# Four projection chunks of a two-layer encoder in Strassen-Winograd form, with the gates kept transposed in DRAM

## The chip, the core and the metric

The kernel runs on one core of a Trainium2 chip. The metric is the device time of one launch, in microseconds (us). The engines are named as the profile names them: PE is TensorE (PEld its weight loads), DVE is VectorE, ACT is ScalarE, POOL is GpSimd, SP is SyncE, which issues every DMA of this kernel. SBUF is the on-chip working memory, PSUM the banks that PE writes to.

## What is computed

Two encoder layers on 1024 tokens of width 1024, all in float32. Each layer normalises, projects once, runs two kinds of attention side by side, gates them, projects back and adds:

```python
proj = rms_norm(x, pre_norm_g[l]) @ w_in[l]              # 1024 x 3328
aq, ak, av, ag, bq, bk, bv, bg = split(proj)             # 512 each, but bk and bv 128 each
oa = diff_attention(aq, ak, av, lam, rel_bias)           # 4 heads, two softmaxes per head
ya = rms_norm(oa, diff_subln_g[l]) * (1 - lam_init) * silu(ag)
yb = gqa_attention(rope(rms(bq)), rope(rms(bk)), bv) * silu(bg)   # 8 query heads on 2 key heads
x = x + rms_norm(concat(ya, yb) @ w_out[l], post_norm_g[l])
```

## The kernel before, in words

**Arithmetic.** Every matmul operand is split into two parts, `hi` (rounded by a copy on ACT) and `lo` (the rest, a subtraction on DVE or POOL). A product is three matmuls: hi by hi, hi by lo, lo by hi (`mm3`). A chunk of 512 projected columns over 1024 rows of depth and 1024 tokens is 8 x 8 x 3 = 192 matmuls of 128 x 512.

**The normalised tokens.** `hT` holds them transposed: for each half of the tokens (`th`) and each half of the depth (`kh`) a pair of hi and lo tiles, 8 tiles in all. With the depth halves as columns and the token halves as rows this is a 2 by 2 block matrix, which the change uses.

**Stages of a layer.** Key/value and query chunks of group B come first, then the chunks `aq` and `ak` (`col_chunk`: the weights are the stationary operand, so the result comes out transposed), then the gates `ag` and `bg` and the values `av` (`tok_chunk`: the tokens are stationary, one PSUM tile per 128 tokens). `gate_post` puts the SiLU of a gate into the row tile `ys[t]`, and for group A multiplies it with `gsub`, the attention norm's gain. Weights are loaded 1 MB at a time into `h` tiles and split into `w` tiles (`w_steps`), the lo half mostly on POOL.

**Attention** goes item by item in `tick`: one tick takes the next item's scores on PE, the reduction of the current one on DVE, its exponential on ACT, later its transposes and its product with the values. `after(d, fn)` puts `fn` off by `d` ticks. The ticks at the start have spare PE work in `fill`: the last two token tiles of `av`, 48 matmuls in five portions, with `av_post` one tick behind (`FD = 1`). The finished rows are multiplied into `ys[t]`, where the gate already lies.

**The end of attention.** `y_transposed(t)` transposes a finished row tile in two halves through the two `pT` banks and splits each. Those of tiles 0 and 1, and the split of the output weights, are laid among the last ticks (`ENDING`); tile t + 2 goes with step t of the first half of the output projection.

**What sets the order.** PE is kept in program order everywhere (`inorder`). In the attention ticks DVE, ACT and POOL are too. Elsewhere a scheduler orders the other engines, SP always, and gives out buffers from pools: 10 `h`, 8 `w`, 6 `e`, 8 `y` tiles, two `pS`, two `pO` and two `pT` places in PSUM. Each engine then runs its list strictly in order: an instruction that waits holds up all behind it.

Of the kernel before, what the change touches and what calls it, by code (L numbers as in the profile page):

```python
# [51 lines left out]
def hybrid_encoder(ctx, tc, x, rel_bias, pre_norm_g, w_in, diff_lambda, diff_subln_g,  # L52
# [208 lines left out]

    def lambdas_of(l, dl):
        lam_init = 0.8 - 0.6 * math.exp(-0.3 * l)
        gsub = cst.tile([P, P], F32, tag="gsub", name=f"gsub{l}")
# [9 lines left out]
        nc.sync.dma_start(gsub, bcast_row(diff_subln_g[l:l + 1, :], P))  # L274
        dve.tensor_scalar(gsub, gsub, 1.0 - lam_init, None, ALU.mult)
        return gsub, neglam

# [25 lines left out]
    def layer(l, hT, ends, given):  # L303
# [7 lines left out]
        bk_d = d_tile([P, 2, 2, S], f"bk_d{l}")  # L311
        bv_d = d_tile([P, 2, NT, P], f"bv_d{l}")

        ys = [None] * NT
        tables = [None]

        def gate_post(t, gi, src):
            if ys[t] is None:
                ys[t] = y_tile()
            dst = ys[t][:, gi * 512:gi * 512 + 512]  # L320
            act.activation(dst, src, AF.Silu)
            if gi == 0:
                d4 = dst.rearrange("p (h c) -> p h c", c=P)
                g4 = gsub.rearrange("p (o c) -> p o c", o=1).broadcast_to([P, 4, P])
                dve.tensor_tensor(d4, d4, g4, ALU.mult)

        def rope_norm(src, t, nh, tab, eps, scale, dst):
            sq = e_tile((P, nh, 64))
# [93 lines left out]
                for fn in side.get(j, ()):  # L422
                    fn()

        def col_chunk(w, scale, store):
            for cb in range(4):
                pt = ps_s()
                for th in range(2):
                    mm_col(pt[:, th * 512:th * 512 + 512], hT[th], w, cb)
                    follow()  # L430
                hi = e_tile(dt=F32R)
                lo = e_tile(dt=F32R)
                act.activation(hi, pt, AF.Copy, scale=scale)
                dve.scalar_tensor_tensor(lo, pt, scale, f(hi), ALU.mult, ALU.subtract)
                store(cb, (f(hi), f(lo)))

        def store_q(h, parts):
            dst = aq_d[h].rearrange("d g (t x k) -> d (g t) x k", t=2, x=4)
            for i in range(2):
                for c in range(2):  # L440
                    nc.sync.dma_start(dst[:, :, 2 * i + c, :],
                                      parts[i][c * 64:c * 64 + 64].rearrange("d (t k) -> d t k", k=P))

        def store_k(h, parts):
            for i in range(2):
                nc.sync.dma_start(ak_d[h, i], parts[i])

        lo4, hi4 = range(4), range(4, 8)
        if l == 0:
# [80 lines left out]
            w_aq, loads, convs = w_steps(wl, C_AQ, on_dve=(1, 3))  # L530
# [4 lines left out]
        else:  # L535
# [6 lines left out]
            w_aq, loads, convs = w_steps(wl, C_AQ, on_dve=(1, 3))  # L542
# [6 lines left out]
        inorder[:] = [nc.tensor]  # L549
        tok_chunk(load_w(wl, C_AG), lambda t, s: gate_post(t, 0, s))  # L550
        tok_chunk(load_w(wl, C_BG), lambda t, s: gate_post(t, 1, s))
        warm = s_tile()
        inorder[:] = [nc.scalar]
        act.activation(warm, neglam, AF.Exp)
        inorder[:] = [nc.tensor]
        w_av = load_w(wl, C_AV)
        tok_chunk(w_av, av_post, tiles=range(NT - 2))

        now = [0]
        trans, parts, later_q, fill = [], [], [], []

        def fill_av(t, cuts):
            box = []

            def part(ks):
                if not box:
                    box.append(ps_o())
                for k in ks:  # L570
                    mm_k(box[0], hT, t, w_av, k)
                if ks[-1] == NK - 1:
                    after(FD, lambda: av_post(t, box[0]))
            fill.extend(lambda ks=ks: part(ks) for ks in cuts)

        for t, cuts in zip((NT - 2, NT - 1), FILL):
            fill_av(t, cuts)

        def after(delay, fn, mid=False):
            later_q.append((now[0] + delay, mid, fn))  # L580
# [96 lines left out]
        def a_out(h, g, aT, r0):  # L677
            box = []

            def part(i):  # L680
                if i == 0:
                    box.append(ps_o())
                pO = box[0][:, 0:256]
                V = values[h]
                for k in (2 * i, 2 * i + 1):
                    pe.matmul(pO, V[:, 0, k, :], aT[0][:, k, :], start=(k == 0), stop=False)
                    pe.matmul(pO, V[:, 0, k, :], aT[1][:, k, :], start=False, stop=False)
                    pe.matmul(pO, V[:, 1, k, :], aT[0][:, k, :], start=False, stop=(k == NK - 1))
                if i == 3:
                    after(0, lambda: finish(box[0]))  # L690

            def finish(pO):
                oT = o_tile((P, 256))
                act.copy(oT, pO[:, 0:256])
                p4 = pO[:, 256:512].rearrange("p (q c) -> p q c", c=P)
                ms = s_tile(2, "oms", 3)
                yv = [ys[g * 2 + qi][:, h * P:(h + 1) * P] for qi in range(2)]
# [49 lines left out]
        def b_out(hp, g, BV, bT, sr):  # L747
# [15 lines left out]
            def finish(j, pO, oT):  # L763
# [17 lines left out]
                def store():  # L781
                    for qi in range(2):
                        for jj in range(2):
                            c0 = 512 + hp * P + jj * 64
                            yv = ys[g * 2 + qi][:, c0:c0 + 64]
                            dve.scalar_tensor_tensor(yv, p4[:, qi, jj * 64:jj * 64 + 64],
                                                     sr[:, jj * 2 + qi:jj * 2 + qi + 1], yv, ALU.mult, ALU.mult)

            return [[lambda j=j, i=i: part(j, i) for i in range(2)] for j in range(2)]

# [10 lines left out]
        def load_ak(h):  # L801
            K = h_tile([P, 2, S], F32R)
            for i in range(2):
# [3 lines left out]
            nc.sync.dma_start(T5, bass.AP(tensor=rows_h.tensor, offset=rows_h.offset + 127,  # L807
                                          ap=[[2047, P], [1, 1920]]))
            return K, T5

        values = {}

# [12 lines left out]
        def all_items():  # L825
            for h in range(4):
# [9 lines left out]
                for g in range(4):  # L836
# [4 lines left out]
                    else:  # L841
                        for fn in half_loads:
                            fn()
                    if g == 0 and 0 < h < 3:
                        state["ak"] = load_ak(h + 1)
                    aT = new_probs()
# [241 lines left out]
```

## Time and profile before

| What | Value |
|---|---|
| Device time, median of three runs | 1461.31 us (1460.11 to 1461.55) |
| Profiled execution, device time | 1459.86 us |
| Its span, first to last instruction | 1457.8 us |
| PE busy | 98% of the span, 8300 matmuls |
| PEld, DVE, ACT, POOL busy | 86%, 57%, 53%, 50% |
| Granted PE clock | 1.00 |
| DMA | 162.45 MB, 111 GB/s on average |

The span is the time from the first to the last instruction; the device time of the same execution is 2.1 us more, for what lies around it. A matmul's end is modelled, so a row of matmuls is better judged by how far apart its members start than by its busy time. A busy share is a mean over stages that have different limits. The stages of the first layer, from the trace: group B's projections until 95 us, `aq` and `ak` until about 186, the gates until about 273, six tiles of `av` until 305, attention until 641, the output projection until 757. The second layer repeats them from there.

### The profile page before, as it was taken

Reading aid. Unit: us, or ns where it says so; the run is one execution under the profiler, and the core shown is the slowest. Engines: PE = TensorE matmul, PEld = TensorE weight load, DVE = VectorE, ACT = ScalarE, POOL = GpSimd, SP = SyncE. Lnnn points to the kernel's source line nnn. Section 1 sums busy time; section 2 is a strip of 40 time slices with the busy share of each in tenths; the row PEclk is TensorE's granted clock in tenths of the full one; section 3 lists DMA queues with packets and bytes.
Section 4 is the critical chain, followed back from the end, with each engine's and each line's share of the span. In section 5 each row is a group of like instructions: output and inputs, shape, how many; then the busy total and the mean of one; then the engine's idle time right before and its main releaser. Section 6 shows DMA issues by size and latency. Waiting matters only on the chain.

```text
span 1457.8 us, 22409 instructions
## 1 busy us (share of the span) xinstructions
PE 1427.4 (98%) x8300; PEld 1248.3 (86%) x8300; DVE 838.0 (57%) x1596; ACT 773.4 (53%) x1508; POOL 736.1 (50%) x740
## 2 busy tenths in 40 slices
PE   6999999999999999999999999999999999999998
PEld 6887888888999999988788888888899999998887
DVE  7861110048888888852786511100688888888423
ACT  5332122148888888852442222111688888888321
POOL 3541122018888888852333422020488888888320
PEclk9999999999999999999999999999999999999999
DMA  6488722165324222041525772124634142311303
GB/s 220 122 203 217 245 87 53 38 187 149 107 66 133 69 78 76 2 145 58 171 93 124 180 203 111 62 51 141 172 89 118 56 109 64 95 59 38 108 29 130
DMA packets 110669, 162.45 MB, mean 111 GB/s; under 512 B 8408, under 2 KB 72408, under 8 KB 108256
## 3 DMA queue, kind: packets, MB, share of 16 engines
q1 hardware_dynamic: 110560, 161.02, 38.2%
q8 instruction: 65, 1.06, 0.3%
q14 instruction: 44, 0.36, 0.1%
HBM read 112.72 MB, written 52.46 MB: 113 GB/s over the span
## 4 chain that ended last, share of the span: by engine, by line
PE 91%; DVE 4%; ACT 2%; issue 1%; POOL 1%; DMA 0%; POOLq 0%; DVEq 0%; SPq 0%; ACTq 0%
PE pS L65 40%; PE pO L65 39%; PE pT L65 13%; DVE y L65 2%; DVE h L65 1%; ACT w L65 1%; ACT e L65 1%; POOL e L65 0%; DVE s L65 0%; DVE w L65 0%; DMA e<-in_pre_norm_g_dram 0%; ACT h L65 0%; POOL w L65 0%; ACT o L65 0%; POOL s L65 0%
## 5 line engine op out<-in xcount | busy, mean ns | idle before, releaser
L65 PE MATMUL pO<-w,h 128*128 128x256 f32 (+1 forms) x3592 | 652.0, 330 | 0.3
L65 PEld LDWEIGHTS pO<-w,h 128*128 128x128 f32 x3592 | 567.1, 189 | 81.3 <-POOL w L65 0.9
L65 PE MATMUL pS<-h,h 128*128 128x512 f32 x1024 | 294.7, 410 | 0.0
L65 POOL TENSOR_TENSOR w<-h,w 128x1024 fp32r<-128x1024 f32 x53 | 127.2, 2421 | 266.8 <-ACT w L65 266.8
L65 PE MATMUL pT<-identr,e 128*128 128x128 f32 x1536 | 200.9, 273 | 1.1 <-DVE w L65 0.9
L65 PEld LDWEIGHTS pS<-h,h 128*128 128x128 f32 x1024 | 174.9, 190 | 24.5 <-ACT e L65 0.4
L65 PE MATMUL pS<-w,h 128*128 128x512 f32 (+1 forms) x912 | 195.3, 370 | 0.0
L65 DVE TENSOR_TENSOR w<-pT,w 128x512 fp32r<-128x512 f32 x256 | 169.7, 684 | 33.5 <-ACT w L65 33.5
L65 POOL TENSOR_SCALAR e<-e,s 128x1024 f32<-128x1024 f32 x64 | 71.8, 1122 | 229.9 <-DVE s L65 229.9
L65 PEld LDWEIGHTS pS<-w,h 128*128 128x128 f32 x912 | 159.3, 190 | 27.9
L65 PEld LDWEIGHTS pT<-identr,e 128*128 128x128 f32 x1536 | 172.6, 140 | 5.6 <-DVE w L65 4.8
L65 PE MATMUL pS<-h,w 128*128 128x512 f32 x768 | 177.0, 391 | 0.0
L65 POOL TENSOR_TENSOR s<-s,mhalf 128x2 f32<-128x2 f32 (+2 forms) x96 | 83.2, 867 | 184.5 <-DVE s L65 181.1
L65 POOL TENSOR_TENSOR w<-e,w 128x512 fp32r<-128x512 f32 x128 | 168.7, 1318 | 10.4
L65 PEld LDWEIGHTS pS<-h,w 128*128 128x128 f32 x768 | 143.5, 188 | 30.4 <-PE pO L65 0.5
L65 ACT CAST w<-pT 128x512 fp32r<-128x512 f32 x256 | 143.6, 587 | 46.2 <-PE pT L65 43.3
L65 DVE TENSOR_REDUCE s<-pS 128x1 f32<-128x1024 f32 x128 | 156.3, 1221 | 15.8 <-PE pS L65 15.0
L65 ACT ACTIVATE e<-e,s 128x1024 f32<-128x1024 f32 x128 | 148.2, 1158 | 22.9 <-DVE s L65 22.1
L65 DVE CUSTOM_DVE_ANT_0 e<-pS,h 128x1024 f32<-128x1024 f32 x128 | 155.6, 1217 | 5.9 <-PE pS L65 5.3
L65 POOL TENSOR_TENSOR e<-e,e 128x1024 f32<-128x1024 f32 x64 | 153.1, 2392 | 5.3
L65 ACT ACTIVATE e<-pS,s 128x1024 f32<-128x1024 f32 x128 | 144.6, 1130 | 6.8 <-issue 5.8
L65 ACT ACTIVATE o<-pO 128x128 f32<-128x128 f32 (+2 forms) x97 | 36.9, 381 | 127.5 <-PE pO L65 116.9
(76 smaller groups left out, 1081.8 us busy)
## 6 DMA issues: line engine op xcount, KB each, us to landing
h<-in_w_in_dram SPq DMA_DIRECT2D x52, 512.0 KB, 4.9
h<-aq_d SPq DMA_DIRECT2D x64, 256.0 KB, 5.2
bq_d<-y SPq DMA_DIRECT2D x64, 128.0 KB, 2.8
aq_d<-e SPq DMA_DIRECT2D x32, 256.0 KB, 4.4
ak_d<-e SPq DMA_DIRECT2D x16, 512.0 KB, 4.4
h<-bq_d SPq DMA_DIRECT2D x32, 256.0 KB, 5.9
h<-ak_d SPq DMA_DIRECT2D x16, 512.0 KB, 7.6
av_d<-e SPq DMA_DIRECT2D x32, 256.0 KB, 2.5
```

Source lines behind the costliest of these rows:

```text
L65: ins = fn(*args, **kw)
```

## The change

`aq`, `ak` and both gates, four chunks per layer, are computed as 2 by 2 block products in Winograd's form of Strassen's scheme. A block product that would take 8 half products (512 tokens by 256 columns over half the depth) takes 7, each of 2 x 4 x 3 = 24 matmuls. So a chunk has 168 matmuls and not 192, all with the weights stationary and the tokens moving.

- **Sums of the tokens** (`sum_steps`): DVE builds four sums `s1` to `s4` of the blocks of `hT` and splits them, during the `av` chunk, which now comes first and whole.
- **Sums of the weights** (`wino_steps`): each chunk's weights come in four loads of 512 KB, DVE forms their sums, and ACT and DVE split seven blocks `wb` of 128 x 4 x 256. POOL has no part in it.
- **Partial results**: products share PSUM (`a` and `b` in `pS` places, `c` in two `pO`), and DVE adds what has been kept in `y` tiles (`added`).
- **Order**: `av`, `ak`, `ag`, `bg`, `aq`. The last two steps of `aq`, 48 matmuls again, become the `fill` at the start of attention. In it `added` is called at once, and the post one tick later.
- **Gates** come out transposed and go to DRAM (`gate_d`) in 16 stores per layer; `load_gates` brings 1 MB per two row tiles back. Attention only copies its rows into `ys[t]`, and `y_transposed` multiplies the transposed rows with the gates (and with `gsub`, now one value per partition).

In all 192 matmuls are gone, 248 DVE and 76 ACT instructions are added (4 of these are table loads), 32 POOL instructions are gone, and 88 DMAs are added.

```diff
-FILL = ((range(0, 3), range(3, 6), range(6, 8)), (range(0, 4), range(4, 8)))
+FILL = (((5, 0, range(0, 3)),), ((5, 0, range(3, 4)), (5, 1, range(0, 2))), ((5, 1, range(2, 4)),),
+        ((6, 0, range(0, 4)),), ((6, 1, range(0, 4)),))
+WLD, WPR = 4, 2
...
+        def wino_steps(c0, post):
...
+            def parted(i, src):
+                wb[i] = w_tile([P, 2, 4, 256])
+                act.copy(wb[i][:, 0], src)
+                dve.tensor_tensor(wb[i][:, 1], src, f(wb[i])[:, 0], ALU.subtract)
...
+            def mm(i, cb, ks):
+                grp, x, first, _ = plan[i]
+                dst, (xh, xl) = bank(grp, cb), blocks[x]
+                cs = slice(cb * P, cb * P + P)
+                for k in ks:
+                    wh, wlo = wb[i][:, 0, k, cs], wb[i][:, 1, k, cs]
+                    on = dict(skip_group_check=not first)
+                    pe.matmul(dst, wh, xh[:, k, :], start=(first and k == 0), stop=False, **on)
+                    pe.matmul(dst, wh, xl[:, k, :], start=False, stop=False, **on)
+                    pe.matmul(dst, wlo, xh[:, k, :], start=False, stop=(k == 3), **on)
+
+            def added(grp, to, base, cb):
+                dst = kept(to, cb)
+                dve.tensor_tensor(dst, bank(grp, cb), kept(base, cb), ALU.add)
+                return dst
...
+            plan = [("a", "a11", True, p1),
+                    ("a", "a12", False, lambda cb: done(cb, 0, bank("a", cb))),
+                    ("b", "s2", True, lambda cb: added("b", "u2", "s1", cb) and None),
+                    ("b", "s3", False, lambda cb: added("b", "u3", "s1", cb) and None),
+                    ("b", "a22", False, lambda cb: done(cb, 1, added("b", "s1", "s1", cb))),
+                    ("c", "s1", True, lambda cb: done(2 + cb, 1, added("c", "u3", "u3", cb))),
+                    ("c", "s4", False, lambda cb: done(2 + cb, 0, added("c", "u2", "u2", cb)))]
...
-        col_chunk(w_aq, -0.125, store_q)
-        col_chunk(load_w(wl, C_AK), 1.0, store_k)
...
-        tok_chunk(load_w(wl, C_AG), lambda t, s: gate_post(t, 0, s))
-        tok_chunk(load_w(wl, C_BG), lambda t, s: gate_post(t, 1, s))
...
+        chunks = [wino_steps(C_AK, post_parts(1.0, store_k)), wino_steps(C_AG, post_gate(0)),
+                  wino_steps(C_BG, post_gate(1)), wino_steps(C_AQ, post_parts(-0.125, store_q))]
...
+        tok_chunk(w_av, av_post, side=side)
...
+        def fill_part(units):
+            for n, cb, ks in units:
+                more = chunks[3][2](n, cb, ks)
+                if more:
+                    after(FD, more)
...
                 def gate():
                     for qi in range(2):
-                        dve.tensor_tensor(yv[qi], p4[:, qi, :], yv[qi], ALU.mult)
+                        dve.tensor_copy(yv[qi], p4[:, qi, :])
...
         def y_transposed(t):
+            if t % 2 == 0 and t + 2 < NT:
+                load_gates(t // 2 + 1)
+            gate = gates[t // 2][:, :, (t % 2) * P:(t % 2) * P + P]
...
-                split(yT[0][:, sl, :], yT[1][:, sl, :], pT)
+                if kh == 0:
+                    dve.scalar_tensor_tensor(gate[:, sl, :], pT, gsub, gate[:, sl, :], ALU.mult, ALU.mult)
+                else:
+                    dve.tensor_tensor(gate[:, sl, :], pT, gate[:, sl, :], ALU.mult)
+                split(yT[0][:, sl, :], yT[1][:, sl, :], gate[:, sl, :])
```

**DVE at the start of attention.** This is DVE's list of the first layer before, from the second group-B reduction on. A row with `<-pS` is a reduction of scores (`ISA` with the bias added, `TENSOR_REDUCE` without), `w<-pT` the lo part of transposed probabilities, `e<-pO` the post of an `av` tile from the fill.

```order
L65 TENSOR_REDUCE s_2405<-pS_2386 128x1
L65 TENSOR_TENSOR e_2427<-pO_2353,e_2427 128x512
L65 ISA e_2444,s_2445<-pS_2407,h_2325 128x1024
L65 ISA s_2445 128x1
L65 TENSOR_TENSOR w_2365<-pT_2432,w_2364 128x4x128
L65 ISA e_2470,s_2471<-pS_2447,h_2325 128x1024
L65 ISA s_2471 128x1
L65 TENSOR_TENSOR e_2479<-pO_2412,e_2479 128x512
```

The same place after the change; `y<-pO` is `added` on a fill product, `e<-y` its post.

```order
L67 SCALAR_TENSOR_TENSOR e_2505<-y_2363,e_2505 128x512
L67 RECIPROCAL s_2440<-s_2442 128x2
L67 SCALAR_TENSOR_TENSOR s_2513<-s_2442,neglam_666,s_2440 128x1
L67 TENSOR_REDUCE s_2518<-pS_2491 128x1
L67 TENSOR_TENSOR y_2333<-pO_2456,y_2333 128x512
L67 SCALAR_TENSOR_TENSOR e_2540<-y_2363,e_2540 128x512
L67 ISA e_2559,s_2560<-pS_2520,h_2428 128x1024
L67 ISA s_2560 128x1
L67 TENSOR_TENSOR y_2333<-pO_2481,y_2333 128x512
L67 TENSOR_TENSOR w_2468<-pT_2547,w_2467 128x4x128
L67 SCALAR_TENSOR_TENSOR e_2584<-y_2333,e_2584 128x512
L67 ISA e_2593,s_2594<-pS_2562,h_2428 128x1024
```

The last fill product (`pO_2481`) is now read ahead of the reduction of `pS_2562`, the scores that PE makes just before that fill; before, the fill's post stood behind the corresponding reduction (`pS_2447`).

**DVE at the end of attention.** Before, from row tile 0's transposed halves (`h<-pT`) on; `w<-h` is the split of the output weights, `o<-o,pO` and `y<-pO` finish the last heads.

```order
L65 TENSOR_TENSOR h_6645<-pT_6646,h_6645 128x512
L65 TENSOR_TENSOR h_6645<-pT_6653,h_6645 128x512
L65 TENSOR_TENSOR o_6408<-o_6408,pO_6593 64x256
L65 RECIPROCAL s_6040<-s_6040 128x4
L65 SCALAR_TENSOR_TENSOR y_1805<-pO_6593,s_6040,y_1805 128x64 x2
```

After, the same place:

```order
L67 SCALAR_TENSOR_TENSOR h_6444<-pT_6783,gsub_665,h_6444 128x4x128
L67 TENSOR_TENSOR h_6782<-h_6444,h_6782 128x512
L67 TENSOR_TENSOR h_6444<-pT_6791,h_6444 128x4x128
L67 TENSOR_TENSOR h_6782<-h_6444,h_6782 128x512
L67 TENSOR_TENSOR o_6543<-o_6543,pO_6728 64x256
L67 RECIPROCAL s_6173<-s_6173 128x4
```

Each half has a product with the gate and then, behind ACT's rounding of it, a subtraction; the rows of the heads (`o`) come behind four operations and not two. Further on, the transposes of row tiles 2 and 3 and of half of tile 4 stand ahead of the first full output tile, where there was tile 2 alone.

**SP at the start of attention.** Before, `aq` had been stored long ago, and the first loads for attention stood among the stores of `av`:

```order
L797 DMA h_2318<-aq_d_88 64x1024 x2
L798 DMA h_2318<-bq_d_91 128x512
L804 DMA h_2322<-ak_d_89 64x2x1024 x2
L274 DMA gsub_7415<-in_diff_subln_g_dram 128x128
L399 DMA av_d_90<-e_2163 128x4x128 x2
```

After, the queries of head 0 are stored, read back, and the keys, the bias rows (`rep_d`) and group B's keys follow, all after the second step of the `aq` chunk:

```order
L937 DMA h_2421<-bq_d_91 128x512
L563 DMA aq_d_88<-e_2290 64x4x128 x4
L563 DMA aq_d_88<-e_2309 64x4x128 x4
L936 DMA h_2421<-aq_d_88 64x1024 x2
L943 DMA h_2425<-ak_d_89 64x2x1024 x2
L946 DMA h_2428<-rep_d 128x1920
L964 DMA h_2430<-bk_d_92 128x2048
```

The first load that attention needs now waits for a store of the chunk that ends just before attention.

More of the change, by code (lines that the diff above doesn't have):

```diff
@@ L263, in lambdas_of @@
         lam_init = 0.8 - 0.6 * math.exp(-0.3 * l)
-        gsub = cst.tile([P, P], F32, tag="gsub", name=f"gsub{l}")
+        gsub = cst.tile([P, 1], F32, tag="gsub", name=f"gsub{l}")
         neglam = cst.tile([P, 1], F32, tag="neglam", name=f"neglam{l}")
@@ L312, in layer, with row_tile @@
         bv_d = d_tile([P, 2, NT, P], f"bv_d{l}")
+        gate_d = d_tile([P, NK, S], f"gate_d{l}")
         ys = [None] * NT
         tables = [None]
-        def gate_post(t, gi, src):
+        def row_tile(t):
             if ys[t] is None:
                 ys[t] = y_tile()
[L320 to L325, printed above, removed]
+            return ys[t]
         def rope_norm(src, t, nh, tab, eps, scale, dst):
@@ L423, in tok_chunk @@
                     fn()
[L425 to L435, printed above, removed]
@@ L437, in store_q, with sum_steps, fresh, tt @@
-        def store_q(h, parts):
-            dst = aq_d[h].rearrange("d g (t x k) -> d (g t) x k", t=2, x=4)
+        blocks = {}
+        def sum_steps():
+            hl = [[[hT[th][i][kh] for i in range(2)] for kh in range(2)] for th in range(2)]
+            (a11, a12), (a21, a22) = hl
+            blocks.update(a11=a11, a12=a12, a22=a22)
+            fs = {}
+            two = lambda j: slice(2 * j, 2 * j + 2)
+            def fresh(n):
+                fs[n] = [y_tile((P, 2, 512)) for _ in range(2)]
+            def tt(dst, x, y, op):
+                for j in range(2):
+                    pick = lambda v: v[j] if isinstance(v, list) else f(v)[:, two(j), :]
+                    dve.tensor_tensor(fs[dst][j], pick(x), pick(y), op)
+            def whole(n, a):
+                fresh(n)
+                tt(n, a[0], a[1], ALU.add)
+            def s1():
+                fresh("s1")
+                tt("s1", fs["s3"], a22[0], ALU.add)
+                tt("s1", fs["s1"], a22[1], ALU.add)
+            def s3s2():
+                tt("s3", fs["s2"], fs["s3"], ALU.subtract)
+                tt("s2", fs["s1"], fs["s2"], ALU.subtract)
+            def s4():
+                fresh("s4")
+                tt("s4", a12[0], fs["s2"], ALU.subtract)
+                tt("s4", fs["s4"], a12[1], ALU.add)
+            def parted(n, home):
+                hi, lo = home([P, 4, 512], F32R), home([P, 4, 512], F32R)
+                for j in range(2):
+                    act.copy(hi[:, two(j), :], fs[n][j])
+                    dve.tensor_tensor(lo[:, two(j), :], fs[n][j], f(hi)[:, two(j), :], ALU.subtract)
+                blocks[n] = (hi, lo)
+            return [lambda: whole("s3", a21), lambda: whole("s2", a11), s1, s3s2, lambda: (s4(), parted("s2", h_tile)),
+                    lambda: parted("s3", w_tile)], [lambda: parted("s1", h_tile), lambda: parted("s4", w_tile)]
@@ L546, in layer @@
         inorder[:] = [nc.tensor]
-        col_chunk(w_aq, -0.125, store_q)
-        col_chunk(load_w(wl, C_AK), 1.0, store_k)
-        inorder[:] = [nc.tensor]
-        tok_chunk(load_w(wl, C_AG), lambda t, s: gate_post(t, 0, s))
-        tok_chunk(load_w(wl, C_BG), lambda t, s: gate_post(t, 1, s))
[L552 to L557, printed above, removed]
+        early, late = sum_steps()
@@ new lines, in layer @@
+        chunks = [wino_steps(C_AK, post_parts(1.0, store_k)), wino_steps(C_AG, post_gate(0)),
+                  wino_steps(C_BG, post_gate(1)), wino_steps(C_AQ, post_parts(-0.125, store_q))]
+        loads = [fn for c in chunks for fn in c[0]]
+        preps = [fn for c in chunks for fn in c[1]]
+        side = {j: [fn] for j, fn in enumerate(early)}
+        side[4] += loads[:2]
+        side[6] = loads[2:WLD] + preps[:1]
+        side[7] = preps[1:WPR]
+        tok_chunk(w_av, av_post, side=side)
@@ new lines, in layer @@
+        tails = []
+        for n in range(7 * len(chunks)):
+            if n < 2:
+                late[n]()
+            if n + WLD < len(loads):
+                loads[n + WLD]()
+            if n + WPR < len(preps):
+                preps[n + WPR]()
+            if n == 21:
+                warm = s_tile()
+                inorder[:] = [nc.scalar]
+                act.activation(warm, neglam, AF.Exp)
+                inorder[:] = [nc.tensor]
+            if n < 26:
+                for cb in range(2):
+                    more = chunks[n // 7][2](n % 7, cb)
+                    follow()
+                    if more:
+                        more()
@@ L561, in layer @@
         now = [0]
         trans, parts, later_q, fill = [], [], [], []
[L564 to L577, printed above, removed]
+        def fill_part(units):
+            for n, cb, ks in units:
+                more = chunks[3][2](n, cb, ks)
+                if more:
+                    after(FD, more)
@@ L579, in after @@
+        fill.extend(lambda units=units: fill_part(units) for units in FILL)
         def after(delay, fn, mid=False):
@@ L696, in finish @@
                 ms = s_tile(2, "oms", 3)
-                yv = [ys[g * 2 + qi][:, h * P:(h + 1) * P] for qi in range(2)]
+                yv = [row_tile(g * 2 + qi)[:, h * P:(h + 1) * P] for qi in range(2)]
                 def norm():
@@ L809, in load_ak, with load_gates @@
             return K, T5
+        gates = {}
+        def load_gates(tp):
+            gates[tp] = h_tile([P, NK, 2 * P])
+            nc.sync.dma_start(gates[tp], gate_d[:, :, tp * 256:tp * 256 + 256])
         values = {}
```

71 lines of the change are left out of this document (62 added, 9 removed).

## Prediction

> **What bounds the kernel now.** I read the page's first part, then the busy time by stage of the first layer, then the chain that ended last, and only then single rows. The page gives the shares:
>
> ```profile
> PE 1427.4 (98%) x8300; PEld 1248.3 (86%) x8300; DVE 838.0 (57%) x1596; ACT 773.4 (53%) x1508; POOL 736.1 (50%) x740
> ```
>
> The stages: `aq` and `ak` (95 to 186 us), both gates and six tiles of `av` (186 to 305), the start of attention with the fill (305 to 323), the ticks, and within them two stretches near their end. The columns are busy time and count of PE, PEld, DVE, ACT, POOL, then the granted clock, the share of the DMA engines and GB/s.
>
> ```profile
> 95.00:186.00 91.00, 91.00 (x408) 74.12 (x407) 18.61 (x24) 20.65 (x25) 22.15 (x10) 1.00 0.74 216
> 186.00:305.00 119.00, 119.00 (x527) 98.59 (x526) 13.19 (x14) 21.48 (x31) 17.24 (x8) 1.00 0.30 92
> 305.00:323.00 18.00, 18.00 (x85) 14.95 (x84) 9.47 (x15) 9.75 (x17) 5.44 (x4) 1.00 0.35 94
> 323.00:641.00 318.00, 314.45 (x2229) 289.97 (x2227) 273.15 (x517) 274.94 (x556) 264.72 (x295) 1.00 0.33 89
> 620.00:630.00 10.00, 8.35 (x68) 7.79 (x67) 6.45 (x14) 8.55 (x20) 7.36 (x11) 1.00 0.41 131
> 630.00:640.00 10.00, 8.78 (x72) 8.17 (x71) 7.91 (x12) 7.35 (x15) 9.84 (x8) 1.00 0.37 134
> ```
>
> In the projections PE has no gap while DVE, ACT and POOL stand idle for 75% and more. In attention everything is nearly full: DVE 86%, ACT 86%, POOL 83%. Near its end PE already waits, 1.65 + 1.22 = 2.87 us in 20. So matmuls are what the projections cost, and time freed there is real; but at the two edges of attention any work put on DVE meets a full engine. The chain gives the price of a matmul, in pieces of start, length and count:
>
> ```profile
> 95.47 5.49 PE pS L65 x24
> 130.94 60.06 PE pS L65 x264
> ...
> 261.72 5.44 PE pS L65 x24
> ```
>
> 5.44 / 24 = 226.7 ns, whichever operand is stationary (60.06 / 264 = 227.5).
>
> **The matmuls removed.** 24 fewer per chunk, four chunks, two layers: 192 x 226.7 ns = 43.5 us. The new ones have the form of `col_chunk`'s, so I keep the price. [...]
>
> **The work put on DVE and ACT in the projections.** Prices (count, busy us, mean ns):
>
> ```profile
> L65 POOL TENSOR_TENSOR w<-h,w 128x1024 fp32r<-128x1024 f32 x53 | 127.2, 2421 | 266.8 <-ACT w L65 266.8
> ...
> L65 ACT CAST w<-h 128x1024 fp32r<-128x1024 f32 x66 | 68.2, 1053 | 58.5 <-PE pS L65 28.5 <-DMA h<-in_w_in_dram 22.6 <-PE pO L65 3.9
> ...
> L65 ACT CAST h<-pT 128x512 fp32r<-128x512 f32 x64 | 34.9, 591 | 6.9 <-PE pT L65 6.0 <-issue 0.6
> ...
> L65 DVE TENSOR_TENSOR y<-pO,e 128x512 f32<-128x512 f32 x31 | 21.4, 690 | 98.2 <-ACT o L65 98.2
> ...
> L65 DVE TENSOR_TENSOR w<-h,w 128x1024 fp32r<-128x1024 f32 x13 | 18.5, 1427 | 1.9 <-POOL w L65 1.9
> ```
>
> A chunk of 168 matmuls lasts 38.1 us. DVE has in it 11 operations of 128 x 1024 (four sums, seven splits) at 1.43, 10 `added` at 0.69 and up to 8 posts at 0.69: 15.7 + 6.9 + 5.5 = 28.1 us. ACT has 7 casts at 1.05 and at most 10 pieces of 0.59: 13.3. The sums of the tokens before the first chunk needs them are 16 additions and four splits: 28.5 us, beside 43.5 us of `av`. Each step's blocks are prepared two steps (10.9 us) ahead. A partial sum has to be read before its bank is added to, and half a step (2.7 us) lies between, against 0.69 plus at most one operation in front. I cost all this at nothing; PE's 38.1 us per chunk hides it. Without that cover DVE would be the bound (a rival below). The 32 POOL splits that go were hidden too. Removing `gsub` from `gate_post` and multiplying no gate in the ticks frees DVE where nothing waits: zero. The 88 added DMAs, `gate_d` among them, go through SP in stages where the share of the DMA engines is 0.30 to 0.74: zero.
>
> **The start of attention, per layer.** First the transfers. `aq` is now the last chunk:
>
> ```profile
> h<-in_w_in_dram SPq DMA_DIRECT2D x52, 512.0 KB, 4.9
> h<-aq_d SPq DMA_DIRECT2D x64, 256.0 KB, 5.2
> ...
> aq_d<-e SPq DMA_DIRECT2D x32, 256.0 KB, 4.4
> ...
> h<-ak_d SPq DMA_DIRECT2D x16, 512.0 KB, 7.6
> ...
> h<-in_w_out_dram SPq DMA_DIRECT2D x16, 512.0 KB, 5.0
> h<-rep_d SPq DMA_DIRECT2D x8, 960.0 KB, 10.8
> ```
> ```profile
> L441 SPq DMA_DIRECT2D aq_d<-e x32: 518/656/2923, 108.0 to 866.9; - x32
> ...
> DMA to landing us min/median/max: 3.3/4.5/15.2
> ```
>
> Count from the start of the second of the five steps of `aq` that run before attention; four of them are left until its first scores, 4 x 5.44 = 21.8 us. Head 0's half of that step is done at 2.7; rounding, subtraction and four issues of SP end at 5.8; landed at 10 (4.4). Eight stores together keep SP until 8.5, so the queries are issued at 10, the keys by 12.2, the bias rows at 12.6. Keys land at 19.8, 2 us early; the bias rows at 23.4, and the first reduction would take them at 22.8. That is 0.6 us late.
>
> Then the fill. These rows of before show one of its ticks (start, length):
>
> ```profile
> 317.78 1.03 PE L65 MATMUL pT<-identr,e 128*128 128x128 f32 x8
> ...
> 319.58 2.91 PE L65 MATMUL pO<-w,h 128*128 128x512 f32 x12
> ...
> 319.89 1.23 DVE L65 CUSTOM_DVE_ANT_0 e<-pS,h 128x1024 f32<-128x1024 f32 x1
> ...
> 323.19 0.69 DVE L65 TENSOR_TENSOR e<-pO,e 128x512 fp32r<-128x512 f32 x1 [2.06 <-ACT e L65]
> ```
>
> DVE reduces the next scores (319.89) while PE runs the 12 fill matmuls, and posts the tile afterwards. By the new order `added` on that product stands ahead of the reduction, so it starts when the fill ends: 322.3 + 0.7, 3.1 us later. Two more posts and the earlier `added` put another 2 x 0.69 in front. Behind DVE wait ACT's exponentials, and PE, whose next scores need the place that the reduction frees. Bounds: nothing, if the two score places and the spare matmuls cover it; 4 x 0.69 + 2 x 0.69 + 2.7 = 6.8 if nothing does; not below nothing, as the 48 matmuls are the same. I take 3.1 + 1.4 = 4.5: after the last fill no spare PE work is left to cover with. A table load now falls behind the first reduction on ACT; the first transposes come four ticks later and hide it. Sum 5.1 per layer.
>
> **The end of attention, per layer.** Row tile 0 before:
>
> ```profile
> 626.28 1.10 PE L65 MATMUL pT<-identr,y 128*128 128x128 f32 x8 [0.51 <-ACT e L65]
> ...
> 627.59 1.29 DVE L65 TENSOR_TENSOR h<-pT,h 128x512 fp32r<-128x512 f32 x2 [1.13 <-ACT h L65]
> ...
> 628.90 0.42 DVE L65 TENSOR_TENSOR o<-o,pO 64x256 f32<-64x256 f32 x1
> ...
> 629.47 0.41 PE L65 MATMUL pO<-identr,o 128*128 128x128 f32 x2 [1.15 <-DVE o L65]
> ```
>
> PE waits there for the head's sum (`o`), which stands behind the tile's two subtractions. After, it stands behind product, subtraction, product, subtraction, and each subtraction waits for ACT's rounding of that product (0.59): about 2 x (0.69 + 0.59) = 2.6 us more per row tile, for tiles 0 and 1 5.2 us. What comes off: the transposes of one and a half more row tiles now stand in these waits; the chain has eight, one row tile, at
>
> ```profile
> 640.29 0.87 PE pT L65 x8
> ```
>
> so 1.5 x 0.87 = 1.3 us of PE work moves into them. Net 3.9. Bounds: a bank is free after one operation and not two, so up to 1.3 us of gain; 10 operations (tiles 2 to 4 too) without cover, 6.9, of loss. I take 3.9, as row 629.47 shows that PE already waits on this very list.
>
> After it, `load_gates` comes two steps ahead. The next layer's `gsub` cannot load until the last row tile has used the old one, and SP holds the second half of the output weights behind it: issued about 1 us into step 5, landed 5 later, then four POOL splits of 2.42; done at 17 us, needed by 20.4. Zero, with 3 us in hand, in the first layer alone.
>
> **Sum.** 43.5 - 2 x (5.1 + 3.9) = 25.5 us. Against this execution's 1459.86 (span 1457.8 and 2.1 around it) that is 1434.4; the median of the runs is 1461.31, 1.45 higher, so 1436. I say 1435.
>
> **The rivals.**
>
> *The edges are covered; the whole saving shows.* For it: fill and PE are busy without a gap until 323 us. Against: 2.87 us of waits at the end already. 1461.3 - 43.5 = 1418, to 1423.
>
> *DVE becomes the bound of the chunks.* For it: two rows of the same split,
>
> ```profile
> 633.20 2.59 DVE L65 TENSOR_TENSOR w<-h,w 128x1024 fp32r<-128x1024 f32 x1 [0.94 <-POOL w L65]
> ...
> 636.65 1.20 DVE L65 TENSOR_TENSOR w<-h,w 128x1024 fp32r<-128x1024 f32 x1
> ```
>
> 2.59 beside a POOL operation, 1.20 without. At 2.59 a chunk would need 11 x 2.59 + 12.4 = 40.9 us against 38.1, 2.8 x 8 = 22 more: 1457. Against: POOL has no work there any more.
>
> *Slower: the store and the load of `aq` in a row.* Place: first scores of each layer. If the store lands as late as the longest (15.2) and the load too, the queries come 16 us after PE is ready: 32 us on top, 1467. It decides from (1461.3 - 1435) / 2 = 13 us per layer. Against: the medians, 4.5 us. The longest ones fell among 4 MB of other writes.
>
> [...]
>
> **How the numbers follow.** Forecast, with its own range 1424 to 1447: 0.67. Covered edges: 0.20. DVE-bound chunks: 0.08. Slower: 0.04, and 0.01 for nothing gained. The range 1418 to 1447 leaves out about 0.1 on each side. Measured against 0.2%, 2.9 us, what a timing of this kernel can tell from no change: faster 0.94, same 0.02, slower 0.04.
>
> **What would show it.** PE x8108; projections from 95 us on about 22 us shorter per layer, steps of 24 matmuls 5.44 apart and no idle PE; at the start of attention 4 to 5 us of idle PE named after DVE; at its end, from row tile 0 to the first output tile, PE idle near 7 us in place of 2.9; first scores with no DMA wait. I am wrong if PE waits for `w` or `y` inside the chunks, if the first scores wait for `h<-aq_d`, or if both edges show no more idle PE than now.

## The result and the profile after

| | Before | After |
|---|---|---|
| Device time, median of four runs | 1460.71 us (1460.02 to 1461.55) | 1520.44 us (1518.82 to 1523.68) |
| Span of the profiled execution | 1457.8 us | 1517.0 us |
| PE busy, matmuls | 1427.4 us, 8300 | 1411.8 us, 8108 |

The ratio is 1.0411, with a 95% interval of 1.0392 to 1.0431: 4.1% slower, where 1435 us had been forecast. The 192 matmuls went, and PE is 15.6 us less busy, but it stands idle for much longer.

Where the 59.2 us of span came from is read from stages with the same work on both sides. The boundaries are starts of PE instructions: the end of group B's chunks, the first scores of attention, the first transposes behind the last scores, and group B's first full query tile of the next layer. Windows of the kernel before (start and end, length, then the columns of the prediction):

```profile
95.22:305.08 209.86, 209.86 (x932) 172.53 (x930) 31.80 (x38) 41.91 (x55) 39.17 (x17) 1.00 0.49 146
305.08:621.74 316.66, 315.99 (x2178) 289.49 (x2177) 268.72 (x507) 269.73 (x539) 252.24 (x282) 1.00 0.32 86
621.74:756.68 134.94, 128.55 (x723) 109.62 (x721) 80.43 (x145) 58.34 (x123) 53.90 (x52) 1.00 0.35 116
756.68:1023.49 266.81, 266.81 (x1244) 222.77 (x1243) 69.96 (x145) 56.85 (x89) 60.48 (x32) 1.00 0.46 127
1023.49:1340.12 316.63, 315.97 (x2177) 289.53 (x2176) 268.84 (x507) 269.91 (x539) 252.27 (x282) 1.00 0.32 85
1340.12:1457.80 117.68, 108.67 (x586) 92.97 (x584) 45.58 (x87) 35.56 (x83) 34.33 (x36) 0.99 0.26 93
```

The same stages of the changed kernel. The projections are in two rows in each layer, the second of them being the Strassen chunks alone, without the part of `aq` that is in the fill:

```profile
95.15:146.85 51.70, 48.64 (x211) 38.60 (x210) 43.52 (x51) 17.22 (x24) 1.64 (x1) 0.97 0.67 196
146.85:327.43 180.58, 151.26 (x625) 114.64 (x624) 80.92 (x89) 52.54 (x68) 0.00 (x0) 1.00 0.39 127
327.43:649.25 321.82, 317.34 (x2177) 291.33 (x2176) 273.79 (x514) 272.72 (x542) 252.98 (x282) 0.99 0.36 99
649.25:788.01 138.76, 129.53 (x722) 109.58 (x721) 89.86 (x161) 60.10 (x123) 54.08 (x52) 1.00 0.39 128
788.01:891.60 103.59, 103.59 (x524) 87.56 (x522) 78.26 (x156) 29.71 (x56) 23.16 (x16) 1.00 0.53 145
891.60:1072.46 180.86, 151.23 (x625) 114.64 (x624) 83.33 (x91) 53.39 (x68) 0.00 (x0) 1.00 0.35 113
1072.46:1394.31 321.85, 316.75 (x2178) 290.58 (x2177) 273.56 (x514) 272.42 (x542) 252.89 (x282) 0.99 0.35 99
1394.31:1517.00 122.69, 110.76 (x586) 94.59 (x584) 55.38 (x103) 37.54 (x83) 34.52 (x36) 0.98 0.31 107
```

| Stage | First layer: change, forecast | Second layer: change, forecast |
|---|---|---|
| projections | 232.28 - 209.86 = +22.4, -21.8 | 284.45 - 266.81 = +17.6, -21.8 |
| attention with its start | +5.2, +5.1 | +5.2, +5.1 |
| end of attention and what follows | +3.8, +3.9 | +5.0, +3.9 |

The two edges came out at the size forecast. The projections lost 44.2 and 39.4 us against the forecast, 83.6 of the 85.4 us by which the time was missed. The rows of the chunks hold 4 x 168 - 48 = 624 matmuls, 141.5 us at 226.7 ns; they take 180.6 and 180.9, so 39.1 and 39.4 us are lost in them. PE's idle time is visible in the second column (151.3 of 180.6). DVE is busy for 80.9 of 180.6 us, 45%: it isn't short of time.

PE and DVE in the middle of the first chunk, from the timeline (start, length, in brackets the idle time before it and what ended it):

```profile
165.05 3.06 PE L67 MATMUL pS<-h,w 128*128 128x512 f32 x12 [0.78 <-DVE y L67]
168.15 0.69 DVE L67 TENSOR_TENSOR y<-pS,y 128x512 f32<-128x512 f32 x1 [3.15 <-PE pS L67]
...
168.89 3.04 PE L67 MATMUL pS<-w,w 128*128 128x512 f32 x12 [0.78 <-DVE y L67]
...
171.96 0.69 DVE L67 TENSOR_TENSOR y<-pS,y 128x512 f32<-128x512 f32 x1 [1.47 <-PE pS L67]
172.71 3.03 PE L67 MATMUL pS<-w,w 128*128 128x512 f32 x12 [0.78 <-DVE y L67]
```

The two engines take turns. DVE reads a half product as soon as its 12 matmuls end (168.11), and PE starts the next half only when that read is done (168.84), though it goes into the other half of the tile. Half a step starts 3.84 us behind the one before it, where 12 x 226.7 ns is 2.72. The prediction had named this as a sign that it is wrong (PE waiting for `w` or `y` inside the chunks). The list of waits sums them for PE (total us, times, longest):

```profile
PE pS L67 <- DVE y L67: 36.7, 40, 1.6
...
PE pS L67 <- ACT y L67: 11.0, 16, 0.8
...
PE pS L67 <- DVE e L67: 5.8, 4, 1.5
PE pS L67 <- ACT e L67: 5.5, 4, 2.0
```

64 waits, 59.0 us idle; and the 12 matmuls behind a wait take 3.84 - 0.78 = 3.06 and not 2.72, 0.3 us more. By this estimate 59.0 + 64 x 0.3 = 78.2, against the 39.1 + 39.4 = 78.5 us that the chunks lost. The groups `c`, whose halves are two `pO` tiles, show no such wait.

The built program has the reason. Here, in words, is what the first matmul of the second half of product `s2` waits for, in the changed kernel and (below) in e1, where the halves are separate tiles:

```
PE MATMUL pS240 <- h209,w231   waits for: DVE TENSOR_TENSOR y241 <- pS240,y233 (the first half's read)
PE MATMUL pT243 <- h209,w231   waits for: the place's use for transposes, long before
```

### The profile page after: what moved, and what is told of

The parts are those of the page before. It is cut to its first block, busy times and chain, and to the rows that moved or that the text cites. A ratio compares the mean times of both kernels' runs of the same rounds, so it can differ in the third digit from the quotient of the medians.

```text
span 1517.0 us, 22632 instructions
## 1 busy us (share of the span) xinstructions
PE 1411.8 (93%) x8108; PEld 1214.3 (80%) x8108; DVE 1051.1 (69%) x1844; ACT 835.1 (55%) x1584; POOL 662.2 (44%) x708
## 5 line engine op out<-in xcount | busy, mean ns | idle before, releaser
L67 PE MATMUL pO<-w,h 128*128 128x256 f32 (+1 forms) x3160 | 550.0, 322 | 0.0
L67 PEld LDWEIGHTS pO<-w,h 128*128 128x128 f32 x3160 | 486.2, 189 | 64.1 <-DVE y L67 0.5
L67 PE MATMUL pS<-h,w 128*128 128x512 f32 x768 | 189.9, 398 | 46.3 <-DVE y L67 24.0
L67 PEld LDWEIGHTS pS<-h,w 128*128 128x128 f32 x768 | 140.4, 188 | 94.5 <-DVE y L67 29.0
L67 POOL TENSOR_TENSOR s<-s,mhalf 128x2 f32<-128x2 f32 (+2 forms) x96 | 85.4, 890 | 185.3 <-DVE s L67 182.0
L67 PE MATMUL pS<-w,h 128*128 128x512 f32 (+1 forms) x576 | 120.6, 367 | 0.0
L67 PEld LDWEIGHTS pS<-w,h 128*128 128x128 f32 x576 | 98.3, 198 | 15.5 <-issue 0.5
L67 ACT ACTIVATE e<-y 128x512 fp32r<-128x512 f32 (+2 forms) x64 | 47.3, 739 | 104.5 <-DVE y L67 77.3
```

The source lines that it names most:

```text
L67: ins = fn(*args, **kw)
```

## Experiments

Each is one kernel. Its ratio is to the kernel before on the same chip (1461.41 us for e1 to e4, 1459.88 for f1 to f4, 1460.01 for g1, 1460.08 for h1). The letters were run on different chips, so a difference between two letters holds to some 1.5 us.

**e1: a PSUM tile for each half.**

```diff
             def bank(grp, cb):
-                if grp == "c":
-                    if (grp, cb) not in ps_:
-                        ps_[grp, cb] = ps_o()
-                    return ps_[grp, cb]
-                if grp not in ps_:
-                    ps_[grp] = ps_s()
-                return ps_[grp][:, cb * 512:cb * 512 + 512]
+                place = dict(a=lambda: ps_s((P, 512)), b=ps_t, c=ps_o)
+                if (grp, cb) not in ps_:
+                    ps_[grp, cb] = place[grp]()
+                return ps_[grp, cb]
```

> The two halves (cb 0 and 1) of each partial product get a PSUM place of their own: group a in two pS places, b in two pT places, c in two pO as it is. All else as in the changed kernel. Theory T (a matmul into one half of a tile waits for the read of the other half, because the wait is kept for the whole tile): PE's waits for y, e and ACT inside the chunks go, chunks start about 38.1 us apart in place of 47.4 to 48.6, and the 39.1 + 39.5 us that the chunks lose in the two layers come back: 1520.4 - 78.6 = 1442 us, 1436 to 1450. The edges of attention and the 5 us of the first layer's av stage stay. Rival D (DVE's amount of work bounds the chunk): chunks stay above 44 us, the time above 1505 us.

Measured: 1457.66 us (1454.14 to 1459.75), ratio to before 0.9976 (0.9965 to 0.9987). One chunk from its start to the next, from the timeline:

```profile
183.11 11.04 PE L67 MATMUL pS<-h,w 128*128 128x512 f32 x48
193.99 5.60 PE L67 MATMUL pT<-h,w 128*128 128x512 f32 x24
...
221.19 11.04 PE L67 MATMUL pS<-h,w 128*128 128x512 f32 x48
```

38.08 us, with no wait inside. The second layer's projections and its attention, as windows:

```profile
754.35:999.38 245.03, 245.03 (x1148) 204.69 (x1146) 160.75 (x246) 83.36 (x124) 22.03 (x16) 1.00 0.46 140
999.38:1328.87 329.49, 319.40 (x2178) 292.79 (x2176) 273.55 (x514) 272.40 (x542) 252.91 (x282) 0.98 0.35 100
```

The projections take 245.03 us, 21.8 less than before, to the tenth what the removed matmuls cost. Theory T holds and D falls: DVE's work is the same. But the time is 15 us above what was expected. Attention now takes 329 us per layer, some 7.4 more than in the changed kernel, and it is at its start:

```profile
268.30 5.32 SPq L560 DMA_DIRECT2D aq_d<-e  x8
...
285.38 5.30 SPq L560 DMA_DIRECT2D aq_d<-e  x8
290.77 0.57 SPq L961 DMA_DIRECT2D h<-bk_d  x1
```
```profile
296.13 2.04 PE L67 MATMUL pS<-h,h 128*128 128x512 f32 x4 [5.64 <-issue]
```

Group B's keys (`bk_d`) stand behind the second eight stores of `aq` in SP's list (it issues nothing from 276.87 to 285.38 us), and the third scores wait for them. `issue` means that the profile names nothing that ended the wait; but the third scores read the tile of this load, and it landed 5.3 us after its issue, at 296.1. Then PE runs at a lower granted clock, 0.53 from 296 to 300 us: 5.6 us of waiting and, by an estimate from that clock, (1 - 0.53) x 4 = 1.9 us of clock come to about the 7.4. The slow chunks had hidden this.

**e2: the same wait in the kernel before.** `aq` and `ak` post by halves:

```diff
             for cb in range(4):
                 pt = ps_s()
-                for th in range(2):
-                    mm_col(pt[:, th * 512:th * 512 + 512], hT[th], w, cb)
-                    follow()
                 hi = e_tile(dt=F32R)
                 lo = e_tile(dt=F32R)
-                act.activation(hi, pt, AF.Copy, scale=scale)
-                dve.scalar_tensor_tensor(lo, pt, scale, f(hi), ALU.mult, ALU.subtract)
+                for th in range(2):
+                    sl = slice(th * 512, th * 512 + 512)
+                    mm_col(pt[:, sl], hT[th], w, cb)
+                    act.activation(hi[:, sl], pt[:, sl], AF.Copy, scale=scale)
+                    dve.scalar_tensor_tensor(lo[:, sl], pt[:, sl], scale, f(hi)[:, sl], ALU.mult, ALU.subtract)
+                    follow()
                 store(cb, (f(hi), f(lo)))
```

> The kernel before, with one edit in aq and ak: the post of each half of a pS tile (128 x 512) comes as soon as that half is done, where one post of 128 x 1024 followed both halves. No matmul and no product is changed. Theory T: in 16 places PE's second half waits for the ACT rounding (0.59) and the DVE subtraction (0.69) of the first half, with 0.4 us to start and restart: 16 x 1.7 = 27 us more, 1488 us, 1478 to 1496. Rival D, or waits that are kept by the half: DVE and ACT are 75% idle there, so no change, 1461 us within 3.

Measured: 1492.28 us, ratio 1.0218 (1.0203 to 1.0233), 30.9 us more in 16 places, where 27 had been expected (its 0.4 us to start and restart agrees with the changed kernel's half steps: 3.84 - 2.72 - 0.69 = 0.43). The list of waits has a new first line, with the count that T gives (15 of them are 1.0 to 1.5 us; before the one of 4.9 DVE had other work in front):

```profile
PE pS L65 <- DVE e L65: 25.9, 16, 4.9
```

So it isn't Strassen's form: a kernel without it pays in the same way for a read of half a tile.

**e3: fewer sums on DVE.** `t3` and `t4` leave out the four sums of the weights.

> The changed kernel without the four sums of the weights in each chunk (blocks 2 to 5 are split from raw weights, so those products are of other numbers); 4 x 1.22 = 4.9 us less on DVE per chunk, 39 us in all. Theory T: the reads that PE waits for are the same, only those that stand behind a sum come sooner: at most 2 us per chunk, 1504 to 1520 us. Rival D: the chunk follows DVE, 4.9 us less in each of eight: 1481 us, 1474 to 1490.

Measured: 1515.20 us, ratio 1.0375 (1.0359 to 1.0390). DVE is busy for 36 us less (1015.1 for 1051.1), and the time falls by 5.2 us. The 40 waits for `y` are still 40, 31.9 us in place of 36.7: T's case.

**e4: the bias products in another place.** `pl = ps_t()` for `ps_o()` in `build_bias_rows`, on top of e1.

> As e1_own_tiles, and the four bias products (4 x 512) of the first layer are put into pT places and not pO. Theory: their waits of 1.08 and 1.98 us, and the lower granted clock behind them (0.66 from 135 to 140 us), come from the place of an av tile whose post stands behind the sums of the tokens on DVE; with another place both go, 3 + 1.8 = about 5 us less than e1_own_tiles. Rival (the sums hold up the bias products wherever they are put): the same as e1_own_tiles within 1 us.

Measured: 1453.91 us, ratio 0.9955 (0.9939 to 0.9972); 3.75 us less than e1, where about 5 had been expected. The first layer's projections in e1 and in e4:

```profile
94.99:286.47 191.48, 188.42 (x836) 154.62 (x834) 123.44 (x139) 70.25 (x91) 1.64 (x1) 1.00 0.53 167
```
```profile
95.19:283.32 188.13, 188.13 (x836) 154.44 (x834) 123.57 (x139) 69.94 (x91) 1.64 (x1) 1.00 0.54 170
```

Both waits are gone, and 188.13 is what the forecast gives, 209.86 - 21.8 = 188.1. The prediction had the sums of the tokens hidden; they held up the post of an `av` tile, and with it the place for a bias product. It is the smaller part of what the projections lost.

**f1: attention's first loads earlier**, on top of e4. `load_bk(0)` and `load_ak(0)` are called behind the first step of `aq`, the first queries behind the second, ahead of the second eight stores.

> As e4_bias_in_pT, and the loads for attention's first items are issued earlier in SP's list: group B's keys, the keys and the bias rows right behind the first step of the aq chunk, the first queries right behind the stores that they need, all ahead of the second eight stores of aq. Theory S (what is left of the gap is SP's list: third scores wait 5.7 us in the first layer and 4.4 in the second for group B's keys, which stand behind eight stores, then run at a lower granted clock): 10.1 + 1.1 + 3 = 14 us less than e4_bias_in_pT, 1440 us, 1435 to 1446. Rival (another load takes its place, the queries or the values): 1450 or more.

Measured: 1437.45 us, ratio 0.9844 (0.9829 to 0.9859), 16.5 us less than e4. Attention is back to 321.6 us in both layers. Theory S holds. f1 moved four loads at once; that the keys were the late one is read from e1's trace. This kernel has no wait in its chunks and the prediction's two edges as they were, and it comes within 2.5 us of the 1435 of the prediction.

**f2 and f3: the edges.** f2 puts each `added` of the fill off by a tick, behind the next reduction:

```diff
...
-                more = chunks[3][2](n, cb, ks)
-                if more:
-                    after(FD, more)
+                later = chunks[3][2](n, cb, ks, True)
+                if later:
+                    after(FD, lambda later=later: later()())
```

> As f1_early_loads, and in the fill each addition of a product to what is kept is put off by one tick, together with its post, so that it stands behind the next reduction in DVE's list. Theory of the prediction (the start loses because the last additions stand ahead of a reduction): the waits of 1.18 and 3.07 us go, with the lower clock behind them: 4 to 6 us per layer, 10 us less than f1_early_loads. Rival (DVE is simply full there, the order is all one): within 2 us of f1_early_loads.

Measured: 1435.26 us, ratio 0.9831 (0.9816 to 0.9846): 2.2 us less than f1, not 10; the rival had said at most 2. The two intervals overlap, but f4 differs from f3 by the same 2.2 us, and the traces show the place. The wait for the reduction (1.2 us in each layer) is gone, the one for `w` stays:

```profile
308.71 1.94 PE L67 MATMUL pT<-identr,e 128*128 128x128 f32 x8 [3.14 <-DVE w L67]
```

f3 puts rounding and subtraction of row tiles 0 and 1 behind the next tick:

```diff
-                split(yT[0][:, sl, :], yT[1][:, sl, :], gate[:, sl, :])
+                if late:
+                    after(0, lambda sl=sl: split(yT[0][:, sl, :], yT[1][:, sl, :], gate[:, sl, :]))
+                else:
+                    split(yT[0][:, sl, :], yT[1][:, sl, :], gate[:, sl, :])
...
```

> As f1_early_loads, and for row tiles 0 and 1 the rounding and the subtraction behind each product with the gate are put off to the end of the next tick, behind the sum of the head that PE waits for. Theory of the prediction (the head's sum stands behind four operations and two roundings on DVE): the wait of 3.37 us falls to about 1.2 in each layer, and the waits for row tile 1 stay: 2 to 4 us per layer, 6 us less than f1_early_loads. Rival (DVE is full, so the halves come late for the first output tile instead): within 2 us of f1_early_loads.

Measured: 1428.75 us, ratio 0.9786 (0.9770 to 0.9802), 8.7 us less than f1, where 6 had been expected. In the profiled executions 4.3 and 3.1 us of it lie behind the two attentions, where the lower clock that f1 has behind its waits (0.50 from 616 to 620 us) is gone too; 1.3 us lie ahead of the first attention, where the two programs are the same, so the edit has about 7.4. PE's waits for the head's sum in f1, and then in f3:

```profile
PE pO L67 <- DVE o L67: 6.7, 2, 3.4
```
```profile
PE pO L67 <- DVE o L67: 1.0, 2, 0.5
```

**f4: both.**

> f2_fill_reads_later and f3_split_later together: 16 us less than f1_early_loads by the theory, 1424 us, 1418 to 1430; the bound of the removed matmuls alone is 1461.3 - 43.5 = 1418. By the rivals within 3 us of f1_early_loads.

Measured: 1426.56 us (1425.56 to 1427.25), ratio 0.9770 (0.9755 to 0.9784): 2.3% faster than before and 6.2% than the change as it was made. It is the fastest kernel here that computes everything. Of the 43.5 us, 33.3 are kept. The start still costs 320.14 - 316.66 = 3.5 us per layer. What stands ahead of the transposed tiles' roundings and subtractions there, from f4's timeline:

```profile
303.50 0.61 ACT L67 ACTIVATE e<-y 128x512 fp32r<-128x512 f32 x1
304.02 1.05 ACT L67 CAST w<-pT 128x512 fp32r<-128x512 f32 x2
304.15 0.69 DVE L67 SCALAR_TENSOR_TENSOR e<-y,e 128x512 fp32r<-128x512 f32 x1 [1.22 <-ACT e L67]
304.76 1.22 DVE L67 TENSOR_REDUCE s<-pS 128x1 f32<-128x1024 f32 x1
305.89 1.28 DVE L67 TENSOR_TENSOR w<-pT,w 128x512 fp32r<-128x512 f32 x2
...
306.72 1.22 PE L67 MATMUL pT<-identr,e 128*128 128x128 f32 x8 [3.14 <-DVE w L67]
```

PE waits for a `pT` place. It comes free when DVE has done the first of the two `w<-pT` (305.89 to 306.57), behind the reduction, behind the last product's post (`e<-y`).

**g1: the posts three ticks later.**

> As f4_both, and each post of a fill product (rounding on ACT, subtraction on DVE) is put off by three more ticks behind its addition. Theory (the wait of 3.1 us for w that is left at the start of attention comes from the post of the last product, whose rounding stands ahead of two roundings of transposed tiles on ACT and whose subtraction stands ahead of a reduction on DVE): it goes, with the lower clock behind it, 3 to 4 us per layer, 1419 us, 1416 to 1423. Rival (the ticks have no room for four posts wherever they stand): 1426.6 us, as f4_both, within 2.

Measured: 1441.88 us, ratio 0.9875 (0.9858 to 0.9891), 15 us more: both theories miss. The 3.1 us wait did fall to 1.2 and 1.2, but a new one came, longest 2.6, and attention takes 328.3 us:

```profile
PE pS L68 <- ACT e L68: 6.4, 4, 2.6
```

A post takes one of the six `e` tiles until its stores have left. In these later ticks the exponentials need them; that they are what runs short was argued from this wait, not tested.

**h1: the last post left out.**

> As f4_both, but the post of the fill's last product (rounding on ACT, subtraction on DVE) is left out; its stores take the parts of the product before it, so the queries of one head's half are of other numbers. The addition, the stores and all matmuls stay. Theory (what is left of the start's loss is that post, which stands ahead of two roundings and a reduction in the lists of ACT and DVE): the 3.1 us wait for w falls under 1 and the time by 3 to 4 us per layer, 1419 us, 1416 to 1423. Rival (the additions and the new lists as a whole are too much for DVE there, whatever single operation goes): at most 1 us per layer, 1424 to 1427.

Measured: 1422.74 us, ratio 0.9743 (0.9727 to 0.9760), 3.8 us less than f4:

```profile
305.02 1.25 PE L67 MATMUL pT<-identr,e 128*128 128x128 f32 x8 [1.28 <-DVE w L67]
```

By the profiles attention takes 318.6 us, so the one post accounts for 1.5 us of the 3.5 in each layer. Part of that is the granted clock, which in f4 is lower behind the wait and in h1 is not (f4, then h1; us, PE busy, clock, DMA share, GB/s):

```profile
308.00:312.00 4.00, 4.00 (x16) 0.57 0.84 300
```
```profile
308.00:312.00 4.00, 3.49 (x20) 1.00 0.97 334
```

The time is just inside the theory's range, but 3.8 us for both layers lies between the two expectations (3 to 4 per layer, and at most 1), and the wait fell to 1.28 and not under 1. The other 2.0 us per layer were not taken apart.

## Why the prediction was wrong

**The matmuls removed: right.** 245.03 against 266.81 us in e1's second layer is 21.78, forecast 21.8. The measured 226.7 ns gives this.

**"A partial sum has to be read before its bank is added to, and half a step lies between": the step that failed.** It was costed at nothing and cost 78.5 us. Each half does have half a step of time, but the program waits by the tile, and both halves were one tile. The argument was about what the data need; it did not look at what PE was made to wait for. The sum of DVE's work, 28.1 us of 38.1, was no guide: DVE was busy for 45% of the time here, and yet PE was held up 64 times, because the reads stood between two matmuls. The rival "DVE becomes the bound of the chunks" had the right sign for the chunks and the wrong cause; e3 and e1 exclude it. Its price of 2.59 us for a split did not come up: in the changed kernel's chunks two such splits took 1.23 us each (163.16 and 169.27), with POOL busy for 0.00 us. And its two rows do not show what POOL does to a split, as POOL had an operation beside both (632.31 to 634.71 and 636.34 to 639.01 us).

**Sums of the tokens hidden: wrong by 5.1 us in the first layer**, 51.70 us where 188.1 - 141.5 = 46.6 were needed. e4 took back 3.35 of it; the rest is, by an estimate from its windows, a lower clock behind the same waits, 3.8 x (1 - 0.65) + 4 x (1 - 0.91) = 1.7 us (134.2 to 138 and 138 to 142 us), which e1 does not show (last section).

**Start of attention: the size right, the parts wrong.** 5.2 against 5.1. In f1 it is 5.0, of which f2 shows 0.7 and 1.6 (first and second layer) to come from the order of `added` and reduction, and h1 another 1.5 from the last post. The prediction had put 4.5 on the first, so that the sum agrees is luck. The sign that it had named is there, 4 to 5 us of idle PE after DVE: 1.18 and 3.09 us in the first layer.

**The transfers: mis-sized, and hidden in the changed kernel.** 0.6 us was allowed, for the bias rows. With chunks at full pace it was 7.4, and the late load was group B's keys. The rival of the store and load in a row came nearest: a load that scores need was late because of the stores of `aq`. But it was late in its issue, behind eight stores on SP's list, and not in its landing (5.3 us), and it was another load. e1's trace and f1 show it.

**End of attention: the size right, one of its two parts shown.** 3.8 us against 3.9 in the first layer, and the row that the prediction pointed at (629.47, 1.15 us behind `o`) became

```profile
659.17 0.41 PE L67 MATMUL pO<-identr,o 128*128 128x128 f32 x2 [3.37 <-DVE o L67]
```

2.2 us more for the first row tile (forecast 2.6); f3 took it away. For the second row tile another 2.6 had been put in, less 1.3 for transposes that move. But in the whole stage PE is idle for 9.2 us where it was for 6.4, which leaves 0.6 beyond that first wait; the other 1.0 of the 3.8 is PE busy for longer. So the net size is in part luck. The second layer lost 1.2 more, at a lower clock (0.69 from 1406 to 1410 us, where the first layer has 1.00).

## What to carry to other kernels

Before you call a read of a partial result hidden, look at what the next matmul waits for in the built program: where two halves shared a tile here, a read of one held up the other. Give each part that is read on its own a tile of its own. And when a stage is sped up, go again through the loads of the next one: 7 us per layer of late keys showed only when the waits ahead of them were gone.

## What the runs showed of the hardware

DVE read one place of PSUM while PE wrote another at full pace: e1's chunks, 168 matmuls, ran 38.08 us with the reads among them, 226.7 ns a matmul. In f2's timeline, with the same tiles, DVE reads a `pT` place from 282.54 to 283.23 us, and PE's 19 matmuls into `pT` around it start 226 ns apart (280.76 to 285.06). e1 changes the tiles alone; the wait on the whole tile was the program's.

The granted clock was lower behind some of PE's gaps and not behind others. Windows of the changed kernel (us, PE busy, clock, DMA share, GB/s), behind gaps of 1.98, 3.09, 3.37 and 3.37 us:

```profile
134.20:138.00 3.80, 3.80 (x12) 0.65 0.93 275
```
```profile
354.00:358.00 4.00, 4.00 (x17) 0.60 0.92 230
```
```profile
660.00:664.00 4.00, 3.99 (x34) 1.00 0.53 185
...
1406.00:1410.00 4.00, 4.00 (x27) 0.69 0.74 262
```

Behind the same gap of 3.37 us it was 1.00 in one layer and 0.69 in the other. And e1 has the bias products' gaps of 1.08 and 1.98 us at the same place, and its clock stays at 1.00, where the changed kernel has 0.65:

```profile
134.00:138.00 4.00, 4.00 (x18) 1.00 0.93 289
```

What decides it was not shown, and the forecast has no term for it. By an estimate from these rows, length x (1 - clock), it cost 1.2 to 1.6 us at each of the three places where the clock was lower, or somewhat more, as the windows do not hold the whole of each slow stretch.
